# Low parts of the weights by one VectorE instruction per 2048-column tile, and differences of the seven products written over the raw weights

## The chip, the core and the metric

The kernel runs on one core of one Trainium2 chip. The metric is the time of one execution on the device, in microseconds (us); the time of a kernel is the median of its runs. PE is TensorE, DVE is VectorE, ACT is ScalarE, POOL is GpSimd, SP is the engine that issues the transfers from HBM.

## What is computed

A decoder trunk of two layers on 256 tokens of width 2048, all in float32. The reference, cut to what matters here:

```python
for i in range(2):
    h = rms_norm(x, attn_norm[i])
    x = x + (mla_mixer(h, ...) if i == 0 else dilated_mixer(h, ...))
    h = rms_norm(x, ffn_norm[i])
    u = h @ w_up                       # 2048 -> 2 x 5632
    c = conv_b + sum(shift(u, j) * conv_w[j] for j in range(3))
    gate, val = c[..., :5632], c[..., 5632:]
    x = x + (silu(gate) * val) @ w_down
return rms_norm(x, final_norm)
```

Layer 0 mixes tokens by latent attention (16 heads, query and key-value ranks of 512), layer 1 by dilated windows (three groups of 16 heads; its input weights alone are 2048 x 18432). Some 500 MB of weights are read once.

## The kernel before

**Splits.** Every float32 matrix product is made of three passes. A weight tile w, [128, 2048] float32 in pool `wst` (three buffers), is split into a high part wh (ScalarE copies it to float32r) and a low part wl = w - wh (VectorE). Pool `wsp` holds five half tiles of 1024 columns for each of them. The activations have a high and a low part too, side by side in one tile of 512 columns. PE adds xh·wh, xl·wh and xh·wl; with the weights as the stationary operand (`proj`, L116 to L131) a high weight block meets 512 moving columns (both parts of the activations) and a low one 256 (the high part alone). `proj` runs all high blocks of a tile and then all low ones, or the other way round, by turns (`runs`, L110), so that low blocks of two tiles follow each other.

`load` (L71 to L100) issues the transfer on SP and then splits half a tile at a time, ACT on L91, DVE on L92:

```python
for a in range(0, n, WS):
    wh = wsp.tile([P, WS], F32R, name="wh", tag="wh")
    wl = wsp.tile([P, WS], F32R, name="wl", tag="wl")
```

The value half of the latent weights is interleaved instead (L97, L98). `load_tok2` (L133) does the same for the values of the dilated layer, where the weights are the moving operand, 512 columns at a time (`proj_tok2`, L157 to L159).

**Order of the work.** The kernel is written as one sequence, and a compiler pass orders each engine's instructions ahead of time: of what is ready in its own reckoning it takes what stands first in the text, gives each tile one of the buffers of its pool, and puts in the waits. A buffer comes free when all instructions that touch its tile are done. On the chip each engine runs its list in order. `unit` (L195) evacuates the result of one projection after the matmuls of the next. `out_proj` and the last `down` start some projections early, with all but their last columns, and finish them when the last head or gate is ready (L366 to L375, L962 to L969).

**The feed-forward.** 44 blocks of 128 hidden columns, two (gate and value) per block, each an upward projection over 16 chunks (`up`, L946). The downward projection runs in three segments of 14, 14 and 16 blocks, 16 output columns each (`down`, L952). In each layer two groups of four blocks (16 to 19 and 30 to 33) are computed with seven block products in place of eight (`seven`, L817): sums and differences of the 2 x 2 blocks of weights and of activations (`forms`). Six of the products run between the projections of `down` (L974, L975): after each output block one entry of the list first(0), second(0), first(1), ... second(7).

- `first(kk)` loads one weight tile (two transfers, L846); w5[:, i, j] are its four blocks of 512 columns, f by c. ACT makes the high part bh of the two raw blocks with i = 0 (L853), DVE the difference t13 in a tile of its own (L854), ACT its high part ch (L855), DVE the low parts bl (L856) and cl (L857); then 12 matmuls, four products (L826 to L828): two with b, then two with c.
- `second(kk)` makes two more differences in the tile t24 (L865, L866; 512 columns each), the second being the last reader of the raw tile apart from L856, splits them (L867, L868) and runs 6 matmuls, two products.
- `third(q)` (L892), two per group, is the seventh product, whose tile holds four chunks as moving blocks of 512 columns; it runs later, between upward projections (L989).

t13 and t24 have one buffer each (`fpool`).

Of the kernel before, what the change touches and what calls it, by code (L numbers as in the profile page):

```python
# [26 lines left out]
P = 128  # L27
T = 256
# [7 lines left out]
WS = 1024  # L36
# [16 lines left out]
def trunk_kernel(tc, x_d, pos_d, gain_d, conv_d, const_d, mask_d, wqa_d, wkva_d, wqb_d, wkvb_d, wo_d,  # L53
                 win_d, dwo_d, wup_d, wdn_d, out_d):
    nc = tc.nc
    with ExitStack() as ctx:
# [3 lines left out]
        wsp = ctx.enter_context(tc.tile_pool(name="wsp", bufs=5))  # L60
# [10 lines left out]
        def load(src, n, tok=0, cuts=None, after=()):  # L71

            w = wst.tile([P, D], F32, name="w", tag="w")
            cuts = cuts or (0, n)
            for a, b in zip(cuts, cuts[1:]):
                nc.sync.dma_start(w[:, a:b], src[:, a:b])
                if after:
                    after[0]()  # L80
                    after = after[1:]
            parts = []
            for a in range(0, n, WS):
                b = min(n, a + WS)
                wh = wsp.tile([P, WS], F32R, name="wh", tag="wh")
                wl = wsp.tile([P, WS], F32R, name="wl", tag="wl")
                if a < tok:
                    steps = [a] + [c for c in cuts if a < c < b] + [b]
                    for c, e in zip(steps, steps[1:]):
                        h, l = wh[:, c - a:e - a], wl[:, c - a:e - a]  # L90
                        nc.scalar.activation(h, w[:, c:e], AF.Copy)  # L91
                        nc.vector.tensor_sub(l, w[:, c:e], h.bitcast(F32))  # L92
                else:
                    for h, t in enumerate((wh, wl)):
                        src2 = w[:, a + h * WS // 2:a + (h + 1) * WS // 2].rearrange("p (k c) -> p k c", c=T)
                        t4 = t.rearrange("p (k s c) -> p k s c", s=2, c=T)
                        nc.scalar.activation(t4[:, :, 0, :], src2, AF.Copy)  # L97
                        nc.vector.tensor_sub(t4[:, :, 1, :], src2, t4[:, :, 0, :].bitcast(F32))  # L98
                parts.append((wh, wl))
            return parts  # L100
# [15 lines left out]
        def proj(w, xs, n, since=0, upto=None, ps=None):  # L116
# [9 lines left out]
            for i in order:  # L126
                for k in ks:
                    w_k = w[k * P // WS][i][:, k * P % WS:k * P % WS + P]
                    nc.tensor.matmul(ps[:, i * T:], w_k, xs[k][:, :(2 - i) * T], start=(k == 0 and i == own),  # L129
                                     stop=(k == n - 1), skip_group_check=(i != own))  # L130
            return ps  # L131

        def load_tok2(srcs, q):  # L133


            w = wst.tile([P, D], F32, name="w", tag="w")
            for i, src in enumerate(srcs):
                nc.sync.dma_start(w[:, i * WS:(i + 1) * WS], src[q // 2][:, q % 2 * WS:(q % 2 + 1) * WS])
            w4 = w.rearrange("p (i k c) -> p i k c", i=2, c=T)
            parts = []  # L140
            for h in range(2):
                wh = wsp.tile([P, WS], F32R, name="wh", tag="wh")
                wl = wsp.tile([P, WS], F32R, name="wl", tag="wl")
                wh4, wl4 = (t.rearrange("p (k i c) -> p i k c", i=2, c=T) for t in (wh, wl))
                src = w4[:, :, 2 * h:2 * h + 2, :]
                nc.scalar.activation(wh4, src, AF.Copy)  # L146
                nc.vector.tensor_sub(wl4, src, wh4.bitcast(F32))  # L147
                parts += [(wh[:, ts(k, 512)], wl[:, ts(k, 512)]) for k in range(2)]
            return parts
# [11 lines left out]
        def proj_short(w, xs, n, off):  # L161

            ps = pp.tile([P, 512], F32, name="pp", tag="pp")
            for k in range(n):
                a = off + k * P
                wh, wl = (t[:, a % WS:a % WS + P] for t in w[a // WS])
                mm3(ps[:, :T], wh, wl, xs[k][:, :T], xs[k][:, T:], k == 0, k == n - 1)
            return ps[:, :T]

        def proj_tok_short(pieces, xs, tt):  # L170
            ps = pp.tile([P, 512], F32, name="pp", tag="pp")
            n = 4 * len(pieces)
            for k in range(n):
                w = pieces[k // 4][k % 4 // 2][:, k % 2 * 2 * T:(k % 2 + 1) * 2 * T]
                mm3(ps[:, :T], xs[k][:, ts(tt, P)], xs[k][:, T + tt * P:T + (tt + 1) * P],
                    w[:, :T], w[:, T:], k == 0, k == n - 1)
            return ps[:, :T]
# [178 lines left out]
        def out_proj(w_d, os, goff, paired=False, then=None):  # L356
# [9 lines left out]
            while steps:  # L366
# [4 lines left out]
                w = load(w_d[b], D, tok=D)  # L371
# [6 lines left out]
            for b in range(len(early), KC):  # L378
                w = load(w_d[b], D, tok=D)
# [40 lines left out]
        def mla():  # L420
# [49 lines left out]
            for k in range(KC):  # L470

                n = 1 if k < 4 else 2
                if k % 4 == 0:
                    w = wst.tile([P, D], F32, name="w", tag="w")
                if k % 2 == 0:
                    wh = wsp.tile([P, WS], F32R, name="wh", tag="wh")
                    wl = wsp.tile([P, WS], F32R, name="wl", tag="wl")
                c = k % 2 * RANK
# [8 lines left out]
                if k % min(n, 2) == 0:  # L487
                    a = k % 4 * RANK
                    nc.scalar.activation(wh[:, c:c + m], w[:, a:a + m], AF.Copy)
                    nc.vector.tensor_sub(wl[:, c:c + m], w[:, a:a + m], wh[:, c:c + m].bitcast(F32))  # L490
# [18 lines left out]
            for b in range(RC):  # L509
                w = load(wkva_d[b], D, tok=D)  # L510
# [11 lines left out]
            w = load(wkva_d[RC], D, tok=D)  # L522
# [578 lines left out]
```

## Time and profile before

| | us |
|---|---|
| median of 3 runs (2686.86 to 2688.9) | 2687.14 |
| the profiled execution | 2689.23 |
| its span, first to last instruction | 2687.4 |
| PE busy (share of the span) | 2669.4 (99%) |
| weight loads of PE busy | 2353.0 (88%) |
| VectorE busy | 2068.8 (77%) |
| ScalarE busy | 1500.9 (56%) |

The profile is of one execution. A busy time is the union of an engine's instructions; matmuls are pipelined, so that the time from one start to the next says more than the duration of one. A group of instructions has its line, its engine, what it writes and reads by the program's names, their shapes, the count, the total and mean time, and the idle time of the engine just before them with what ended it. wl and wh in a row of `second` or `first` are the halves called bl, cl, dl and bh, ch, dh here; t is t13 or t24.

### The profile page before, as it was taken

The page shows a single profiled execution, that of the slowest core. Times are in us where ns is not written, and L with a number is a line of the kernel's source. Part 1 is how long each engine was busy: PE and PEld are TensorE (multiplying, and loading weights), DVE is VectorE, ACT ScalarE, POOL GpSimd, SP SyncE. Part 2 cuts the span into 40 slices and gives each one's busy share as a digit, 9 for nine tenths or more (in the row PEclk, how much of TensorE's full clock was granted, in tenths as well). Part 3 has the DMA queues.
Part 4 walks back from the last instruction along what each step waited for, and adds up shares of the span by engine and source line. Part 5 has one row for each costly group of instructions (what it writes and reads, how often), then busy time and mean ns, then how long its engine had stood idle before and what let it go on. Part 6 is the DMA issues. An engine that isn't in the chain of part 4 may idle for free.

```text
span 2687.4 us, 39711 instructions
## 1 busy us (share of the span) xinstructions
PE 2669.4 (99%) x15301; PEld 2353.0 (88%) x15301; DVE 2068.8 (77%) x3591; ACT 1500.9 (56%) x2254; POOL 24.4 (1%) x39
## 2 busy tenths in 40 slices
PE   9999999999999999999999999999999999999998
PEld 7998888888888888888888888888888888888887
DVE  7987888789788767676576667667688878978875
ACT  6775666566556554444454454444566646655653
POOL 2000000000000000000000000000000000000000
PEclk9999999999999999999999999999999999999999
DMA  6435555665665555544544544544555566566553
GB/s 236 142 134 204 188 188 184 210 218 186 200 221 192 196 188 191 185 173 170 191 167 165 198 161 173 188 173 160 189 188 189 188 204 219 187 197 225 189 188 126
DMA packets 125902, 501.98 MB, mean 187 GB/s; under 512 B 10000, under 2 KB 60560, under 8 KB 85136
## 3 DMA queue, kind: packets, MB, share of 16 engines
q1 hardware_dynamic: 125424, 499.26, 54.1%
q8 instruction: 120, 1.97, 0.3%
q14 instruction: 70, 0.57, 0.1%
q10 hardware_dynamic: 288, 0.18, 0.0%
HBM read 497.30 MB, written 2.10 MB: 186 GB/s over the span
## 4 chain that ended last, share of the span: by engine, by line
PE 69%; issue 27%; DVE 1%; DMA 1%; POOL 0%; POOLq 0%; ACT 0%; DVEq 0%; SPq 0%; ACTq 0%
PE pp L129 50%; PE pp L157 3%; PE pp L158 3%; PE pp L159 3%; PE pp L104 1%; PE pp L106 1%; PE pp L105 1%; DMA w<-in_wup 1%; PE po L754 1%; PE ps L717 1%; PE ps L826 0%; PE ps L827 0%; PE ps L828 0%; DVE wl L92 0%; PE ps L104 0%
## 5 line engine op out<-in xcount | busy, mean ns | idle before, releaser
L92 DVE TENSOR_TENSOR wl<-w,wh 128x1024 fp32r<-128x1024 f32 (+2 forms) x770 | 912.8, 1193 | 363.8 <-ACT wh L91 234.5
L91 ACT ACTIVATE wh<-w 128x1024 fp32r<-128x1024 f32 (+2 forms) x770 | 793.7, 1034 | 513.2 <-PE pp L129 282.0
L129 PE MATMUL pp<-xs,wh 128*128 128x512 f32 x3904 | 917.5, 390 | 0.0
L129 PEld LDWEIGHTS pp<-xs,wh 128*128 128x128 f32 x3904 | 723.7, 188 | 144.6
L129 PEld LDWEIGHTS pp<-xs,wl 128*128 128x128 f32 x3904 | 487.8, 192 | 9.8
L129 PE MATMUL pp<-xs,wl 128*128 128x256 f32 x3904 | 496.0, 284 | 0.0
L129 PE MATMUL pp<-a,wh 128*128 128x512 f32 x1920 | 454.5, 390 | 0.0
L129 PEld LDWEIGHTS pp<-a,wh 128*128 128x128 f32 x1920 | 357.6, 188 | 72.6
L129 PEld LDWEIGHTS pp<-a,wl 128*128 128x128 f32 x1920 | 244.2, 191 | 9.3 <-DVE wl L92 1.6
L129 PE MATMUL pp<-a,wl 128*128 128x256 f32 x1920 | 248.9, 283 | 0.8 <-DVE wl L92 0.8
L205 ACT ACTIVATE lo<-pp 128x256 f32<-128x256 f32 x241 | 92.5, 384 | 137.2 <-PE pp L129 136.8
L147 DVE TENSOR_TENSOR wl<-w,wh 128x1024 fp32r<-128x1024 f32 x96 | 116.2, 1218 | 62.5 <-ACT wh L146 50.3
L934 DVE SCALAR_TENSOR_TENSOR cv<-upad,convs,cv 128x256 f32<-128x256 f32 x288 | 138.1, 481 | 25.7 <-ACT cv L930 21.5
L146 ACT ACTIVATE wh<-w 128x1024 fp32r<-128x1024 f32 x96 | 101.6, 1058 | 97.0 <-PE pp L158 50.0
L157 PE MATMUL pp<-wh,xs 128*128 128x512 f32 x384 | 150.0, 391 | 0.0
L159 PE MATMUL pp<-wl,xs 128*128 128x512 f32 x384 | 149.4, 389 | 0.0
L158 PE MATMUL pp<-wh,xs 128*128 128x512 f32 x384 | 149.4, 389 | 0.0
L930 ACT ACTIVATE cv<-upad,convs 128x256 f32<-128x256 f32 x144 | 86.1, 599 | 96.8 <-DVE upad L944 95.0
L354 DVE TENSOR_TENSOR x<-x,pp 128x256 f32<-128x256 f32 x256 | 105.2, 414 | 8.2 <-PE pp L129 7.1
L854 DVE TENSOR_TENSOR t<-w 128x1024 f32<-128x1024 f32 x32 | 39.2, 1224 | 82.5 <-DMA w<-in_wup 82.5
L207 DVE TENSOR_TENSOR sum<-pp,lo 128x256 f32<-128x256 f32 x241 | 100.8, 418 | 0.5 <-ACT lo L205 0.4
L159 PEld LDWEIGHTS pp<-wl,xs 128*128 128x128 f32 x384 | 72.1, 188 | 15.1
(291 smaller groups left out, 2630.3 us busy)
## 6 DMA issues: line engine op xcount, KB each, us to landing
w<-in_wup SPq DMA_DIRECT2D x144, 1024.0 KB, 4.8
w<-in_win SPq DMA_DIRECT2D x96, 1024.0 KB, 4.8
w<-in_wdn SPq DMA_DIRECT2D x64, 896.0 KB, 4.6
w<-in_win SPq DMA_DIRECT2D x96, 512.0 KB, 4.1
w<-in_wup SPq DMA_DIRECT2D x64, 512.0 KB, 5.1
w<-in_wdn SPq DMA_DIRECT2D x32, 1024.0 KB, 4.9
w<-in_wo SPq DMA_DIRECT2D x16, 1024.0 KB, 4.8
w<-in_dwo SPq DMA_DIRECT2D x16, 1024.0 KB, 4.8
```

The costliest lines, as they stand in the source:

```text
L91: nc.scalar.activation(h, w[:, c:e], AF.Copy)
L92: nc.vector.tensor_sub(l, w[:, c:e], h.bitcast(F32))
L129: nc.tensor.matmul(ps[:, i * T:], w_k, xs[k][:, :(2 - i) * T], start=(k == 0 and i == own), stop=(k == n - 1), skip_group_check=(i != own))
L146: nc.scalar.activation(wh4, src, AF.Copy)
L147: nc.vector.tensor_sub(wl4, src, wh4.bitcast(F32))
L157: nc.tensor.matmul(ps, xh, wh, start=k == 0, stop=False)
L158: nc.tensor.matmul(ps, xl, wh, start=False, stop=False)
L159: nc.tensor.matmul(ps, xh, wl, start=False, stop=k == KC - 1)
L205: nc.scalar.activation(t, ps[:, T:], AF.Copy)
L207: nc.vector.tensor_add(u, ps[:, :T], t)
L354: nc.vector.tensor_add(x, x, a)
L934: nc.vector.scalar_tensor_tensor(o, v, convs[:, cw + j:cw + j + 1], o, op0=ALU.mult, op1=ALU.add)
```

## The change

- The pool of half tiles is replaced by three high tiles and two low tiles of 2048 columns. `load` splits with two ScalarE instructions and one VectorE instruction over the whole tile. The latent value weights are split like all others and no longer interleaved.
- `load_tok2` and `third` split in the order in which the weights lie, so that a moving block of 512 columns is 2 x 256 or 4 x 128 columns of the tile.
- In `first` the difference t13 is written over the two raw blocks with j = 0, after bh and bl; one of the two differences of `second` is made in `first`, and both lie in the two blocks with j = 1. The high parts b and c are one high tile; their low parts are one tile `scr` with one buffer. `second` takes a high and a low tile. Products 6 and 4 change halves accordingly.
- `sums` and `make_forms` use the same `scr` tile in place of t13 and t24.

```diff
-        wsp = ctx.enter_context(tc.tile_pool(name="wsp", bufs=5))
+        whi = ctx.enter_context(tc.tile_pool(name="whi", bufs=3))
+        wlo = ctx.enter_context(tc.tile_pool(name="wlo", bufs=2))
...
+        def raw_tile():
+            return wst.tile([P, D], F32, name="w", tag="w")
+
+        def high_tile():
+            return whi.tile([P, D], F32R, name="wh", tag="wh")
+
+        def low_tile():
+            return wlo.tile([P, D], F32R, name="wl", tag="wl")
+
+        def halves(w, wh, wl, n):
+
+            for a, b in ((0, D // 2), (D // 2, n)):
+                nc.scalar.activation(wh[:, a:b], w[:, a:b], AF.Copy)
+            nc.vector.tensor_sub(wl[:, :n], w[:, :n], wh[:, :n].bitcast(F32))
+
+        def load(src, n):
+
+            w, wh, wl = raw_tile(), high_tile(), low_tile()
+            nc.sync.dma_start(w[:, :n], src[:, :n])
+            halves(w, wh, wl, n)
+            return wh, wl
...
+            halves(w, wh, wl, D)
+            blocks = [t.rearrange("p (i k c) -> p k i c", i=2, c=T) for t in (wh, wl)]
+            return [tuple(t[:, k] for t in blocks) for k in range(4)]
...
+            def scratch(dtype):
+                return fpool.tile([P, 4 * HALF], dtype, name="scr", tag="scr")
...
-                products = {1: ("a11", 0, 0), 2: ("a12", 0, 1), 5: ("s1", 1, 0), 7: ("s3", 1, 1), 6: ("s2", 2, 0),
-                            4: ("a22", 2, 1)}
+                products = {1: ("a11", 0, 0), 2: ("a12", 0, 1), 5: ("s1", 1, 0), 7: ("s3", 1, 1), 6: ("s2", 2, 1),
+                            4: ("a22", 2, 0)}
...
+                    w, wh, bl = raw_tile(), high_tile(), scratch(F32R)
...
-                    t13 = fpool.tile([P, 2 * HALF], F32, name="t13", tag="t13")
-                    t24 = fpool.tile([P, 2 * HALF], F32, name="t24", tag="t24")
-                    (bh, bl), (ch, cl) = pieces = [pair() for _ in range(2)]
+                    (bh, ch), (bl, cl) = ([t[:, ts(i, 2 * HALF)] for i in range(2)] for t in (wh, bl))
 
                     nc.scalar.activation(as4(bh), w5[:, 0], AF.Copy)
-                    nc.vector.tensor_sub(as4(t13), w5[:, 1], w5[:, :, 0])
-                    nc.scalar.activation(ch, t13, AF.Copy)
                     nc.vector.tensor_sub(as4(bl), w5[:, 0], as4(bh).bitcast(F32))
-                    nc.vector.tensor_sub(cl, t13, ch.bitcast(F32))
+                    t13 = w5[:, :, 0]
+                    nc.vector.tensor_sub(t13, w5[:, 1], t13)
+                    nc.scalar.activation(as4(ch), t13, AF.Copy)
+                    nc.vector.tensor_sub(w5[:, 1, 1], w5[:, 1, 1], w5[:, 0, 0])
+                    nc.vector.tensor_sub(as4(cl), t13, as4(ch).bitcast(F32))
...
-                    nc.vector.tensor_sub(t4[:, 0], w5[:, 1, 1], t1[:, 0])
-                    nc.vector.tensor_sub(t4[:, 1], t4[:, 0], w5[:, 0, 1])
-                    nc.scalar.activation(dh, t24, AF.Copy)
-                    nc.vector.tensor_sub(dl, t24, dh.bitcast(F32))
+                    dh, dl = high_tile()[:, :2 * HALF], low_tile()[:, :2 * HALF]
+
+                    nc.vector.tensor_sub(w5[:, 0, 1], w5[:, 1, 1], w5[:, 0, 1])
+                    t42 = w5[:, :, 1]
+                    nc.scalar.activation(as4(dh), t42, AF.Copy)
+                    nc.vector.tensor_sub(as4(dl), t42, as4(dh).bitcast(F32))
...
-                    for h in range(2):
-                        bh, bl = pair()
-                        as4 = lambda t: t.rearrange("p (k f c) -> p k f c", k=2, f=4)
-                        nc.scalar.activation(as4(bh), w5[:, 2 * h:2 * h + 2], AF.Copy)
-                        nc.vector.tensor_sub(as4(bl), w5[:, 2 * h:2 * h + 2], as4(bh).bitcast(F32))
-                        for k in range(2):
-                            product(3, "s4", 4 * q + 2 * h + k, bh[:, ts(k, HALF)], bl[:, ts(k, HALF)])
+                    halves(w, wh, wl, D)
+                    blocks = [t.rearrange("p (f k c) -> p k f c", f=4, k=4) for t in (wh, wl)]
+                    for k in range(4):
+                        product(3, "s4", 4 * q + k, *(t[:, k] for t in blocks))
```

## Rows read from the trace of the kernel before

**Rows 1.** The page, parts 1 and 2: busy time by engine, granted clock in 40 slices.

```profile
PE 2669.4 (99%) x15301; PEld 2353.0 (88%) x15301; DVE 2068.8 (77%) x3591; ACT 1500.9 (56%) x2254; POOL 24.4 (1%) x39
...
PEclk9999999999999999999999999999999999999999
```

**Rows 2.** Waits of PE and of its weight loads: total us, times, longest.

```profile
PE po L275 <- DVE acc L249: 1.6, 1, 1.6
...
PEld pp L828 <- DVE wl L868: 1.8, 4, 0.5
...
PEld pp L129 <- DVE wl L92: 1.6, 4, 0.5
```

**Rows 3.** Chain that ended last, its longest piece: start us, us, what.

```profile
188.41 84.75 PE pp L129 x488
```

**Rows 4.** Groups by line and shape: count, busy us and mean ns, idle before.

```profile
L129 PE MATMUL pp<-xs,wh 128*128 128x512 f32 x3904 | 917.5, 390 | 0.0
L92 DVE TENSOR_TENSOR wl<-w,wh 128x1024 fp32r<-128x1024 f32 x698 | 849.1, 1221 | 362.9 <-ACT wh L91 233.6 <-PE pp L129 124.0 <-issue 0.5
...
L129 PEld LDWEIGHTS pp<-xs,wh 128*128 128x128 f32 x3904 | 723.7, 188 | 144.6
...
L157 PE MATMUL pp<-wh,xs 128*128 128x512 f32 x384 | 150.0, 391 | 0.0
...
L354 DVE TENSOR_TENSOR x<-x,pp 128x256 f32<-128x256 f32 x256 | 105.2, 414 | 8.2 <-PE pp L129 7.1
...
L854 DVE TENSOR_TENSOR t<-w 128x1024 f32<-128x1024 f32 x32 | 39.2, 1224 | 82.5 <-DMA w<-in_wup 82.5
...
L853 ACT ACTIVATE wh<-w 128x1024 fp32r<-128x1024 f32 x32 | 34.0, 1063 | 33.4 <-PE pp L129 28.3 <-ACT wh L91 3.4 <-ACT cv L930 1.6
...
L92 DVE TENSOR_TENSOR wl<-w,wh 128x512 fp32r<-128x512 f32 x8 | 5.5, 688 | 0.8 <-ACT wh L91 0.8
```

**Rows 5.** Timeline of PE, 451 to 465 us (start, us, what).

```profile
451.02 0.40 PE L826 MATMUL ps<-wh,xs 128*128 128x512 f32 x1
...
453.77 3.33 PE L129 MATMUL pp<-a,wh 128*128 128x512 f32 x14
456.94 1.84 PE L129 MATMUL pp<-a,wl 128*128 128x256 f32 x14
458.61 0.40 PE L826 MATMUL pp<-wh,forms 128*128 128x512 f32 x1
...
464.85 0.40 PE L826 MATMUL ps<-wh,xs 128*128 128x512 f32 x1
```

**Rows 6.** Timeline of DVE, 450 to 466 us.

```profile
450.21 1.23 DVE L854 TENSOR_TENSOR t<-w 128x1024 f32<-128x1024 f32 x1 [0.80 <-DMA w<-in_wup]
...
457.10 0.68 DVE L865 TENSOR_TENSOR t<-w,t 128x512 f32<-128x512 f32 x1
457.81 0.69 DVE L866 TENSOR_TENSOR t<-t,w 128x512 f32<-128x512 f32 x1
458.42 1.22 DVE L856 TENSOR_TENSOR wl<-w,wh 128x1024 fp32r<-128x1024 f32 x1
...
465.58 1.23 DVE L854 TENSOR_TENSOR t<-w 128x1024 f32<-128x1024 f32 x1 [3.01 <-DMA w<-in_wup]
```

**Rows 7.** Timeline of SP, the transfer of the next products' weights.

```profile
459.67 0.93 SPq L846 DMA_DIRECT2D w<-in_wup  x2
```

**Rows 8.** Busy us by engine in one round of the products (PE, PEld, DVE, ACT).

```profile
451.02:464.85 13.83, 13.83 (x77) 11.99 (x76) 11.52 (x17) 7.20 (x8) 0.00 (x0) 1.00 0.67 210
```

**Rows 9.** Windows of 2 us after a wait of PE; the clock follows POOL.

```profile
50.00:52.00 2.00, 2.00 (x16) 2.00 (x16) 1.86 (x5) 1.57 (x3) 0.70 (x1) 0.82 0.00 0
52.00:54.00 2.00, 2.00 (x12) 2.00 (x11) 1.95 (x5) 0.00 (x0) 0.00 (x0) 0.50 0.65 138
54.00:56.00 2.00, 2.00 (x14) 1.91 (x14) 1.89 (x6) 1.31 (x3) 0.00 (x0) 0.83 0.62 255
```

**Rows 10.** Windows of the latent-attention heads.

```profile
80.00:100.00 20.00, 20.00 (x174) 20.00 (x174) 18.96 (x68) 15.52 (x50) 0.00 (x0) 1.00 0.54 186
```

More of the change, by code (lines that the diff above doesn't have):

```diff
@@ L35 @@
 HEADS = 16
-WS = 1024
 NG = 3
@@ L68, in trunk_kernel @@
         pso = ctx.enter_context(tc.tile_pool(name="pso", bufs=1, space=PSUM))
[L71 to L100, printed above, removed]
+        def raw_tile():
[13 more added lines that the diff above has]
+            return wh, wl
         def mm3(ps, ah, al, bh, bl, first, last):
@@ L127, in proj @@
                 for k in ks:
-                    w_k = w[k * P // WS][i][:, k * P % WS:k * P % WS + P]
-                    nc.tensor.matmul(ps[:, i * T:], w_k, xs[k][:, :(2 - i) * T], start=(k == 0 and i == own),
+                    nc.tensor.matmul(ps[:, i * T:], w[i][:, ts(k, P)], xs[k][:, :(2 - i) * T], start=(k == 0 and i == own),
                                      stop=(k == n - 1), skip_group_check=(i != own))
@@ L133, in load_tok2 @@
         def load_tok2(srcs, q):
-            w = wst.tile([P, D], F32, name="w", tag="w")
+            w, wh, wl = raw_tile(), high_tile(), low_tile()
             for i, src in enumerate(srcs):
-                nc.sync.dma_start(w[:, i * WS:(i + 1) * WS], src[q // 2][:, q % 2 * WS:(q % 2 + 1) * WS])
-            w4 = w.rearrange("p (i k c) -> p i k c", i=2, c=T)
-            parts = []
-            for h in range(2):
[L142 to L149, printed above, removed]
+                nc.sync.dma_start(w[:, ts(i, D // 2)], src[q // 2][:, ts(q % 2, D // 2)])
+            halves(w, wh, wl, D)
+            blocks = [t.rearrange("p (i k c) -> p k i c", i=2, c=T) for t in (wh, wl)]
+            return [tuple(t[:, k] for t in blocks) for k in range(4)]
         def proj_tok2(w, pss_, xs, q):
@@ L164, in proj_short, with proj_tok_short @@
             for k in range(n):
-                a = off + k * P
-                wh, wl = (t[:, a % WS:a % WS + P] for t in w[a // WS])
+                wh, wl = (t[:, off + k * P:off + (k + 1) * P] for t in w)
                 mm3(ps[:, :T], wh, wl, xs[k][:, :T], xs[k][:, T:], k == 0, k == n - 1)
             return ps[:, :T]
-        def proj_tok_short(pieces, xs, tt):
+        def proj_tok_short(w, xs, tt, off):
             ps = pp.tile([P, 512], F32, name="pp", tag="pp")
[L172 to L176, printed above, removed]
+            for k in range(RC):
+                wh, wl = (t[:, off + k * T:off + (k + 1) * T] for t in w)
+                mm3(ps[:, :T], xs[k][:, ts(tt, P)], xs[k][:, T + tt * P:T + (tt + 1) * P], wh, wl,
+                    k == 0, k == RC - 1)
             return ps[:, :T]
@@ L370, in out_proj @@
                 b = len(early)
-                w = load(w_d[b], D, tok=D)
+                w = load(w_d[b], D)
                 early.append((w, proj(w, os, KC, upto=HEADS - 2)))
@@ L473, in mla @@
                 if k % 4 == 0:
[L474 to L478, printed above, removed]
+                    w, wh, wl = raw_tile(), high_tile(), low_tile()
+                c = k % 4 * RANK
                 if k % n == 0:
@@ L520, in keep_kpe @@
                 split_to(kpes, kpe)
-            w = load(wkva_d[RC], D, tok=D)
+            w = load(wkva_d[RC], D)
             flush()
@@ L539, in project @@
             def project(j):
-                wq = load(wqb_d[j], 3 * RC * P, tok=D)
-                wkv = load(wkvb_d[j], 4 * RC * P, tok=WS)
+                wq = load(wqb_d[j], 3 * RC * P)
+                wkv = load(wkvb_d[j], 4 * RC * P)
                 h = {}
@@ L583, in project @@
                     unit(lambda: proj_short(wkv, st["skvn"], RC, e * RC * P), lambda ps, e=e: keep_k(e, ps))
[L584 to L585 removed]
+                unit(lambda: proj_tok_short(wkv, st["skvn"], 0, 2 * RC * P), keep_v0)
+                unit(lambda: proj_tok_short(wkv, st["skvn"], 1, 2 * RC * P), keep_v1)
                 return h
@@ L828, in product @@
                     nc.tensor.matmul(ps[i], xh, wl, start=False, stop=(kk == KC // 2 - 1))
-                def pair():
-                    wh = wsp.tile([P, WS], F32R, name="wh", tag="wh")
-                    wl = wsp.tile([P, WS], F32R, name="wl", tag="wl")
-                    return wh, wl
                 raw = {}
@@ L878, in sums @@
                 def sums():
-                    a = fpool.tile([P, 2 * HALF], F32, name="t13", tag="t13")
-                    b = fpool.tile([P, 2 * HALF], F32, name="t24", tag="t24")
-                    u[1, 2], u[2, 2], u[1, 1], u[2, 1] = a[:, :HALF], a[:, HALF:], b[:, :HALF], b[:, HALF:]
+                    a = scratch(F32)
+                    u[1, 2], u[2, 2], u[1, 1], u[2, 1] = (a[:, ts(i, HALF)] for i in range(4))
                     nc.scalar.activation(u[1, 2], ps[1], AF.Copy)
```

39 lines of the change are left out of this document (17 added, 22 removed).

## The prediction

> **What bounds the kernel now.** I read the busy shares first: PE is busy 99% of the span, VectorE (DVE) 77%, and the granted clock is at full speed in every slice [rows 1]. Busy alone doesn't say that PE sets the time, so I read its waits next: everything that PE or its weight loads waited for from the two lines that make low parts, L92 and L868, is 1.6 and 1.8 us, a few tenths at a time [rows 2]. Then the chain that ended last: its longest piece is 488 matmuls in 84.75 us with nothing else in it, 174 ns each; they are half 512 and half 256 columns wide, so a pair takes 347 ns [rows 3]. PE issues matmuls back to back, and the other engines only have to stay ahead. So what the change can give is what PE waits for, about 3.4 us; what it can cost is whatever makes PE wait.
>
> The change touches two things that keep the others ahead: how many weight tiles are in flight, and what must follow what around the seven products. There a round (first and second of one kk, each followed by one block of the downward projection over 14 chunks) takes 13.83 us, PE busy throughout, VectorE 11.52 [rows 8]. With t = 0 at the first product: first(kk) to 2.75, a projection to 7.59, second(kk) to 8.98, a projection to 13.83 [rows 5].
>
> **The change part by part.**
>
> *One VectorE instruction per tile.* 1024 columns take 1221 ns, 512 take 688 [rows 4]: 1.041 ns a column and 155 ns fixed. There were 898 low-part instructions (770 on L92, 16 on L98, 96 on L147, 16 on L906); there will be 445, one per tile: 309 full L92 tiles, 64 of 1792 columns, 16 in the latent heads, 48 value tiles, 8 third products. 453 x 0.155 = 70 us of VectorE work go, but off the path: PE's 3.4 us of waits are the whole cover to be lifted. I take 0, ends 0 and -3.4.
>
> *Later first use.* A low part now exists only when its whole tile is done: 155 + 2048 x 1.041 = 2.29 us after its high part instead of 1.22. In the plain upward stage a projection is 16 x 347 ns = 5.55 us and a low tile is freed a whole projection before its successor is read, so the 2.29 us lie beside PE. Nothing, as long as VectorE isn't late; if it is, 1.07 us per late tile.
>
> *Two low tiles, three high tiles* in place of five halves of each. Cover is lost where a low tile is held longer or freed just before the next is due: (a) the tiles started early before the last head or last gate is ready (L366 to L375, L962 to L969), which keep both low tiles until their last columns run, four places; (b) the fourth projection after each group of seven, whose low tile comes free only one third(q) (12 matmuls, about 2.75 us) before it is due, four places; (c) the latent heads, where VectorE is busy 18.96 of 20 us [rows 10] and the wkv tile's low part now has to fall between the end of one head pair and the fourth unit of the next (36 matmuls of about 0.12 us plus attention). Each costs between 0 and one whole low part, 2.29 us: 4 + 4 + 7 places, 0 to 34 us. I take 0.2 us each, nearer to nothing, since today's waits of this kind are at most 0.5 us [rows 2]: 3 us.
>
> *Differences in place.* Same count of VectorE and ScalarE instructions, but a new order: the 1-3 difference (L854) overwrites raw weights, so it now waits for the high part of the raw weights and its low part (L853, L856). Today it runs straight off the transfer, at 450.21 for products that start at 464.85, over 14 us ahead [rows 5, 6], and this lead hides the wait for the weights that VectorE shows (3.01 us a round, 82.5 in all [rows 4, 6]). And the raw tile, today given back after L856 at 459.64, whereupon the next transfer starts at 459.67 and lands at 465.58, 5.9 us later [rows 6, 7], is now held until second(kk)'s low part. What is queued behind: on SP the next projection's transfer, on VectorE everything after bl.
>
> The round by hand, from rows 4 and 6: the second low tile frees at t = 7.59 when the middle projection ends; the next projection's low part (1792 columns, 2.02 us) ends at 9.6, one residual pair (2 x 0.41) at 10.4. Then bl 1.22, difference 1.22, ch on ScalarE 1.06, cl 1.22: 15.1. The next first(kk) starts at 13.83 and its ninth matmul, eight times 0.229 later (2.75 / 12), is the first to read cl: 15.66. Slack 0.5 us. If the short subtraction (0.69) and dh (1.06) fit beside ch, dl follows cl at once, and the next transfer (5.9) and high part (1.06) are done before 10.4: no wait. If one more residual pair falls into the chain (0.83), PE waits 0.3 us. If the following projection's low part is put ahead of second(kk), dl ends at 15.1 + 2.02 + 0.69 + 1.06 + 1.22 = 20.1; a transfer that has to wait for that raw tile lands at 26.0, 12.2 of the next round, cl is done at 18.0, and PE waits 2.3 us. Ends 0 (PE has next to no wait here to give back) and 2.3 us a round, 32 rounds, 28 of them with a predecessor: 0 to 64 us. I take 0.3, nearer to the first, because in today's order L865 and L866 of second() already run before L856 of first() [rows 6], so the subtractions are issued as soon as they can be: 32 x 0.3 = 10 us.
>
> *Strided moving operands.* Value tiles and third products now give PE 2 x 256 and 4 x 128 columns in place of 512 in a row. No row shows such a read; every 512-column matmul takes 390 or 391 ns [rows 4]. I take 0. As an upper end, each further piece costs the part of a matmul that doesn't shrink with its columns: 14 matmuls of 512 columns go in 3.17 us and 14 of 256 in 1.67 [rows 5], 226 and 119 ns each, so 107 for 256 columns and 12 fixed; (1152 + 3 x 96) x 12 = 17 us.
>
> Sum: 0 + 3 + 10 = +13. The profiled execution took 2689.23 us (span 2687.4), 2.1 over the median of 2687.14; added to the median: **2700 us**. 0.2%, about what measuring this kernel can tell from no change, is 5.4 us.
>
> **The rivals.**
>
> *No change* (2684 to 2692). The chain keeps its 0.5 us, the subtractions fit beside ch, and the edges are covered; a low tile taken from whichever frees first helps. For it: VectorE has 2.3 us idle in a round [rows 8], and the change lightens it by 0.3. Against: the lead of 14 us is gone. 2687. Chance 0.36.
>
> *The raw tile's loop* (the 2.3 us case). Place: the transfer on SP behind dl. It decides once dl ends later than about t = 17.3, so that transfer and high part run past 10.4. 28 x 2.3 + 3 = 2754; partly, 2720 to 2754. A wait of 1.6 us can also cost clock: after the one of that length before L275 [rows 2] the granted clock is 0.82, 0.50 (1.2 of 2.4 GHz) and 0.83 in three windows of 2 us [rows 9], 1.7 us of issue lost; on top of every round this would be 48 more. Chance 0.14.
>
> *PE reads pieces slower*: 2687 + 17 + 13 = 2717. Nothing for it but that nothing rules it out. Chance 0.04.
>
> *Faster: VectorE was the real limit.* If PE's 99% were padding, the 70 us taken off VectorE would return in part; half would give 2652. The rows speak against it: weight loads last 188 ns [rows 4] under matmuls issued 226 ns apart, so their idle share is only the wider matmul streaming. If only the 3.4 us of waits come back it is 2684, which counts as no change. Chance 0.04.
> The Trainium skill (Perfetto Trace Analysis, Identifying the Most-Contended Engine) says that matmul busy time is no measure of headroom and that the weight-load share is; by that the 88% here would leave PE 334 us, and this rival would be likely. The piece of 488 matmuls without a wait disagrees, so I follow the row.
>
> **How the numbers follow.** Forecast (small waits at the products, 2693 to 2720) 0.42; with the loop 0.14 and the slower reads 0.04, slower is 0.60; no change 0.36; faster 0.04. The range, 2684 to 2735, takes in no change, the forecast with the slower reads, and the smaller half of the loop; it leaves out faster and the full loop. The forecast case alone: 2693 to 2720.
>
> **What would show it.** Right: L92's successor at about 2.29 us, VectorE busy down by up to 70 us, rounds of 14.1 to 14.3 us with PE waiting for the low or high part of the difference, and the transfer of in_wup issued right after second()'s low part. Wrong: rounds still at 13.83 (no change), rounds of 15 us or more with the transfer in the chain or the clock below 1 (the loop), or value-tile matmuls issued over 235 ns apart (reads). A span under 2680 would overturn the reading that PE bounds.

## The result, and the profile after the change

The changed kernel takes **2691.91 us** (median of 19 runs, 2690.18 to 2693.96); the kernel before, beside it, 2687.14 (19 runs, 2684.73 to 2689.73): ratio 1.0018, 95% interval 1.0012 to 1.0024. It is 4.8 us slower, just under the 5.4 us that the prediction called no change, and 8 us under its 2700. The profiled execution took 2693.96 us, its span is 2692.2, also 4.8 more than before.

The page's busy times and clock [rows 1]:

```profile
PE 2670.5 (99%) x15301; PEld 2352.7 (87%) x15301; DVE 2015.0 (75%) x3138; ACT 1431.1 (53%) x2246; POOL 19.7 (1%) x39
...
PEclk9999999999999999999999999999999999999999
```

VectorE has 453 instructions fewer, as counted, and 53.8 us less to do; PE is as busy as it was. Groups by line and shape [rows 4]:

```profile
L84 DVE TENSOR_TENSOR wl<-w,wh 128x2048 fp32r<-128x2048 f32 x373 | 853.4, 2288 | 287.4 <-PE pp L119 130.1 <-PE pp L141 110.2 <-ACT v L663 24.8
...
L139 PE MATMUL pp<-wh,xs 128*128 128x512 f32 x384 | 150.1, 391 | 0.0
...
L84 DVE TENSOR_TENSOR wl<-w,wh 128x1792 fp32r<-128x1792 f32 x64 | 129.2, 2019 | 0.0
```

The whole low part takes the 2.29 and 2.02 us worked out, and a value tile's matmul, now reading 2 x 256 columns, 391 ns as before. PE's and the weight loads' waits [rows 2]:

```profile
PE pp L119 <- DVE wl L84: 5.3, 6, 1.5
...
PEld pp L119 <- DVE wl L84: 6.3, 8, 1.8
```

Low parts that PE waits for are few again, but longer: the weight loads' waits reach 1.8 us where the longest was 0.5, PE's own 1.5. The next three views are one round of the seven products. PE's timeline (start, us, what) [rows 5]:

```profile
495.54 0.40 PE L809 MATMUL ps<-wh,xs 128*128 128x512 f32 x1
...
497.83 0.39 PE L811 MATMUL pt<-scr,forms 128*128 128x512 f32 x1
...
498.28 3.34 PE L119 MATMUL pp<-a,wh 128*128 128x512 f32 x14
...
509.36 0.40 PE L809 MATMUL ps<-wh,xs 128*128 128x512 f32 x1
```

From the first product of this round (495.54) to that of the next (509.36) it is 13.82 us: no round is late. 497.83 is the first matmul that reads cl. VectorE's timeline [rows 6]:

```profile
494.39 2.02 DVE L84 TENSOR_TENSOR wl<-w,wh 128x1792 fp32r<-128x1792 f32 x1
496.33 1.22 DVE L835 TENSOR_TENSOR scr<-w,wh 128x1024 fp32r<-128x1024 f32 x1
...
499.69 1.23 DVE L846 TENSOR_TENSOR wl<-w,wh 128x1024 fp32r<-128x1024 f32 x1 [0.88 <-ACT wh L845]
502.75 1.22 DVE L829 TENSOR_TENSOR scr<-w,wh 128x1024 fp32r<-128x1024 f32 x1 [1.83 <-ACT wh L828]
503.89 2.02 DVE L84 TENSOR_TENSOR wl<-w,wh 128x1792 fp32r<-128x1792 f32 x1
```

L829 is bl, L835 cl, L846 dl; cl is done at 497.55, 0.28 us before it is read. A window of one round's length [rows 8]:

```profile
496.23:510.06 13.83, 13.83 (x75) 11.99 (x74) 11.12 (x13) 6.65 (x7) 0.00 (x0) 1.00 0.65 208
```

VectorE is busy 11.12 us of it. SP's timeline [rows 7]:

```profile
496.44 0.93 SPq L824 DMA_DIRECT2D w<-in_wup  x2
...
510.27 0.93 SPq L824 DMA_DIRECT2D w<-in_wup  x2
```

The transfer starts as the neighbouring projection's low part ends (494.39 + 2.02 = 496.41), and 3.3 us before dl begins. So it seems to take that projection's raw tile and not to wait for its predecessor's; experiments 1 and 6 bear this out.

Where the 4.8 us come from, by the same PE instruction in both traces (the first matmul of a round's third product, `pt`): the seven rounds from the first round's mark to the last's take 96.82, 98.17, 96.79 and 98.49 us in the four groups before, 96.83, 96.83, 96.85 and 96.83 after, **2.9 us less**. The stretches outside take 3.0 (up to the first group), 0.9, 2.0, 1.2 and 0.6 us more, **7.7 us**. The waits shown next make 5.7 of it. The other 2.0 are not explained; a second profile of the kernel before (experiment 10) differs from the first by as much there. PE's timeline there, all stretches between single rows left out:

```profile
77.27 0.38 PE L95 MATMUL pp<-sqh,wl 128*128 128x256 f32 x1 [0.42 <-DVE k L321]
...
192.56 1.94 PE L119 MATMUL pp<-a,wl 128*128 128x256 f32 x14 [1.45 <-DVE wl L84]
...
583.00 1.22 PE L119 MATMUL pp<-xs,wl 128*128 128x256 f32 x8 [0.54 <-DVE wl L84]
...
813.03 2.17 PE L119 MATMUL pp<-xs,wl 128*128 128x256 f32 x16 [0.56 <-DVE wl L84]
...
927.61 1.66 PE L119 MATMUL pp<-a,wl 128*128 128x256 f32 x12 [1.24 <-DVE wl L84]
...
2263.55 1.69 PE L119 MATMUL pp<-xs,wl 128*128 128x256 f32 x12 [1.07 <-DVE wl L84]
...
2606.63 1.54 PE L119 MATMUL pp<-a,wl 128*128 128x256 f32 x11 [0.44 <-DVE wl L84]
```

192.56, 927.61 and 2606.63 are the prediction's place (a), tiles started early; 583.00, 813.03 and 2263.55 its place (b), the fourth projection after a group. VectorE's timeline at the first of each:

```profile
189.65 0.42 DVE L321 TENSOR_TENSOR a<-pt,a 128x256 fp32r<-128x256 f32 x1
190.21 2.29 DVE L84 TENSOR_TENSOR wl<-w,wh 128x2048 fp32r<-128x2048 f32 x1
...
579.27 1.00 DVE L907 SCALAR_TENSOR_TENSOR cv<-upad,convs,cv 128x256 f32<-128x256 f32 x2 [1.66 <-ACT cv L903]
580.31 0.42 DVE L912 TENSOR_TENSOR cv<-cv 128x256 f32<-128x256 f32 x1
580.66 2.29 DVE L84 TENSOR_TENSOR wl<-w,wh 128x2048 fp32r<-128x2048 f32 x1
```

PE goes on as soon as the whole 2.29 us are over. The low part could not start earlier at 190.21: both low tiles were held by the early projections, and PE came to the last low block of the first of them only at 189.89. At 580.66 it could have: by the order of use its tile was free from about 579.7 on (PE read the projection before from 577.63 for 2.08 us), but L907 and L912, which had waited for ScalarE, stand ahead of it in VectorE's list.

### The profile page after: what moved, and what is told of

The parts are those of the page before. It is cut to its first block, busy times and chain, and to the rows that moved or that the text cites. A ratio compares the mean times of both kernels' runs of the same rounds, so it can differ in the third digit from the quotient of the medians.

```text
span 2692.2 us, 38702 instructions
## 1 busy us (share of the span) xinstructions
PE 2670.5 (99%) x15301; PEld 2352.7 (87%) x15301; DVE 2015.0 (75%) x3138; ACT 1431.1 (53%) x2246; POOL 19.7 (1%) x39
## 4 chain that ended last, share of the span: by engine, by line
PE 68%; issue 27%; DVE 2%; DMA 1%; ACT 0%; POOLq 0%; POOL 0%; DVEq 0%; ACTq 0%
PE pp L119 49%; PE pp L139 3%; PE pp L141 3%; PE pp L140 3%; DVE wl L84 1%; PE pp L95 1%; PE pp L97 1%; PE pp L96 1%; PE ps L694 1%; DMA w<-in_wup 1%; PE po L731 1%; PE ps L97 0%; PE ps L95 0%; PE ps L96 0%; PE ps L809 0%
## 5 line engine op out<-in xcount | busy, mean ns | idle before, releaser
L84 DVE TENSOR_TENSOR wl<-w,wh 128x2048 fp32r<-128x2048 f32 (+2 forms) x445 | 996.7, 2240 | 289.4 <-PE pp L119 130.1
L83 ACT ACTIVATE wh<-w 128x1024 fp32r<-128x1024 f32 x890 | 884.7, 1031 | 410.3 <-PE pp L119 136.1
L119 PEld LDWEIGHTS pp<-xs,wl 128*128 128x128 f32 x3904 | 486.7, 192 | 14.1 <-DVE wl L84 4.2
L907 DVE SCALAR_TENSOR_TENSOR cv<-upad,convs,cv 128x256 f32<-128x256 f32 x288 | 138.2, 482 | 61.4 <-ACT cv L903 55.7
L829 DVE TENSOR_TENSOR scr<-w,wh 128x1024 fp32r<-128x1024 f32 x32 | 39.2, 1226 | 61.5 <-ACT wh L828 61.5
L139 PEld LDWEIGHTS pp<-wh,xs 128*128 128x128 f32 x384 | 72.1, 188 | 14.8
L140 PEld LDWEIGHTS pp<-wh,xs 128*128 128x128 f32 x384 | 72.1, 188 | 14.8
```

The costliest lines, as they stand in the source:

```text
L83: nc.scalar.activation(wh[:, a:b], w[:, a:b], AF.Copy)
L84: nc.vector.tensor_sub(wl[:, :n], w[:, :n], wh[:, :n].bitcast(F32))
L119: nc.tensor.matmul(ps[:, i * T:], w[i][:, ts(k, P)], xs[k][:, :(2 - i) * T], start=(k == 0 and i == own), stop=(k == n - 1), skip_group_ch ...
L139: nc.tensor.matmul(ps, xh, wh, start=k == 0, stop=False)
L140: nc.tensor.matmul(ps, xl, wh, start=False, stop=False)
L829: nc.vector.tensor_sub(as4(bl), w5[:, 0], as4(bh).bitcast(F32))
```

## The experiments

Two theories stood against each other for the 7.7 us: whole tiles (a low part is one long instruction, of which nothing can be read before its end), or the number of low buffers and the order. For the rounds the question was why the 10 us were not there. Each ratio is to the kernel before, run beside the experiment; its median was 2685.33 us beside experiments 1 to 4, 2686.94 beside 5 to 8 and 2687.45 beside 9 and 10.

**1. The low part in two instructions, same tiles.**

```diff
             for a, b in ((0, D // 2), (D // 2, n)):
                 nc.scalar.activation(wh[:, a:b], w[:, a:b], AF.Copy)
-            nc.vector.tensor_sub(wl[:, :n], w[:, :n], wh[:, :n].bitcast(F32))
+                nc.vector.tensor_sub(wl[:, a:b], w[:, a:b], wh[:, a:b].bitcast(F32))
```

> The changed kernel, but the low part of each loaded tile is made by two VectorE instructions of one half each; the two whole low tiles stay. Theory A (the loss is PE waiting for the last 1.07 us of a low part that now comes in one piece): the six waits of PE for low parts (1.45, 0.54, 0.56, 1.24, 1.07 and 0.44 us in the profile of the changed kernel, 5.3 in all) shrink by up to 1.07 each to about 0.4 in all, and the time falls by 4 to 5 us to about 2687. Theory B (the loss is that a whole low tile has to come free first): the waits move by a few tenths only, and the time stays at 2690 to 2692. VectorE is busier by about 60 us in either case.

Measured: 2698.47 us (5 runs), 1.0052 (1.0040 to 1.0064). The edge waits shrank (at the first place from 1.45 to 0.38), and yet it is slower: the rounds now last up to 14.9 us, 9.6 us more in the four groups. The timeline of one of them, all engines:

```profile
481.56 0.93 SPq L824 DMA_DIRECT2D w<-in_wup  x2
...
493.19 1.22 DVE L84 TENSOR_TENSOR wl<-w,wh 128x1024 fp32r<-128x1024 f32 x1
...
494.33 1.22 DVE L835 TENSOR_TENSOR scr<-w,wh 128x1024 fp32r<-128x1024 f32 x1
...
495.46 0.96 DVE L84 TENSOR_TENSOR wl<-w,wh 128x768 fp32r<-128x768 f32 x1
495.61 0.50 PE L811 MATMUL pt<-scr,forms 128*128 128x512 f32 x1 [0.81 <-DVE scr L835]
...
496.48 0.93 SPq L824 DMA_DIRECT2D w<-in_wup  x2
...
500.88 1.06 ACT L828 ACTIVATE wh<-w 128x1024 fp32r<-128x1024 f32 x1 [0.67 <-DMA w<-in_wup]
```

The order puts cl between the two halves of the neighbour's low part, so that its raw tile comes free 1.1 us later; the transfer starts when it does (495.46 + 0.96 = 496.42), ACT waits for the transfer, and bl, cl and the next round follow. Two transfers stand 14.92 us apart here, 13.83 in the changed kernel. So the round can be late in the way the prediction priced, through a raw tile, but the neighbour's. cl's place alone is not enough for it, as experiment 2 shows.

**2. Low tiles of half the size, four in place of two.**

```diff
-        wlo = ctx.enter_context(tc.tile_pool(name="wlo", bufs=2))
+        wlo = ctx.enter_context(tc.tile_pool(name="wlo", bufs=4))
...
-            return wlo.tile([P, D], F32R, name="wl", tag="wl")
+            return wlo.tile([P, D // 2], F32R, name="wl", tag="wl")
...
-            nc.vector.tensor_sub(wl[:, :n], w[:, :n], wh[:, :n].bitcast(F32))
+                nc.vector.tensor_sub(wl[i][:, :b - a], w[:, a:b], wh[:, a:b].bitcast(F32))
```

> The changed kernel with four low half tiles of 1024 columns in place of two whole ones (the same memory), each filled by an instruction of its own and freed by itself. Theory A and theory B both expect the six waits for low parts to go (5.3 us) and the time to fall to 2684 to 2687; if two low tiles are not the reason (the three high tiles, or the order of ScalarE's copies, or the reads of the moving operand in pieces), the time stays at 2690 to 2692.

Measured: 2685.58 us (median of 12 runs, 2684.93 to 2686.26 but for one of 8047.19), 1.0001 (0.9992 to 1.0010). Of the edge waits one is left (1.03 us at 196.49), and all rounds but one (14.12) last 13.83. The same bytes, released and filled in halves, cost nothing: it is the size of the unit that costs, not the space. VectorE in a round that is on time:

```profile
721.30 1.23 DVE L84 TENSOR_TENSOR wl<-w,wh 128x1024 fp32r<-128x1024 f32 x1 [0.72 <-ACT wh L83]
...
723.05 1.22 DVE L854 TENSOR_TENSOR scr<-w,wh 128x1024 fp32r<-128x1024 f32 x1
724.18 0.95 DVE L84 TENSOR_TENSOR wl<-w,wh 128x768 fp32r<-128x768 f32 x1
```

cl (L854) stands between the neighbour's halves here too. But one half of a projection's low part is made between bl and cl, where experiment 1 has three: the two halves of the other projection are made ahead of bl (those at 728.42 and 730.52 ahead of bl at 731.72).

**3. The order of high and low blocks after the third products.** `proj` alternates high-low and low-high; this starts it with high blocks after a third product.

```diff
                         product(3, "s4", 4 * q + k, *(t[:, k] for t in blocks))
+                    state["run"] = 0
```

> The changed kernel, but the projection after each third product begins with its high part. If the three waits of 0.54, 0.56 and 1.07 us after the groups of seven come from a low tile that is freed one third product before it is due, they go, and the time falls by about 2 us to 2690; the waits at 192.6, 927.6 and 2606.6 us stay. If something else is late there, nothing changes.

Measured: 2695.80 us (5 runs), 1.0040 (1.0028 to 1.0052). The three waits of place (b) are gone, but everything behind alternates the other way round, and places (a) pay for it. PE's timeline at one:

```profile
915.22 2.08 PE L119 MATMUL pp<-a,wl 128*128 128x256 f32 x16
...
919.68 3.43 PE L119 MATMUL pp<-a,wl 128*128 128x256 f32 x16 [1.80 <-DVE wl L84]
```

The windows behind it (busy us of PE, PEld, DVE, ACT and POOL, then the granted clock, the share of the DMA engines, GB/s):

```profile
920.00:922.00 2.00, 2.00 (x12) 2.00 (x11) 2.00 (x4) 2.00 (x4) 0.00 (x0) 0.54 0.69 193
922.00:924.00 2.00, 2.00 (x10) 1.82 (x9) 2.00 (x4) 0.92 (x3) 0.00 (x0) 0.61 0.81 336
```

The wait is 1.80 us instead of 1.24, and behind it the granted clock is near its lower level, 1.2 of 2.4 GHz: the 16 matmuls take 3.43 us, where the 16 before the wait take 2.08.

**4. The differences over the raw weights alone.** The kernel before, five half tiles each, with the change's `first` and `second` (its own low tiles for b and c kept).

```diff
-                    nc.vector.tensor_sub(as4(t13), w5[:, 1], w5[:, :, 0])
-                    nc.scalar.activation(ch, t13, AF.Copy)
                     nc.vector.tensor_sub(as4(bl), w5[:, 0], as4(bh).bitcast(F32))
-                    nc.vector.tensor_sub(cl, t13, ch.bitcast(F32))
+                    t13 = w5[:, :, 0]
+                    nc.vector.tensor_sub(t13, w5[:, 1], t13)
+                    nc.scalar.activation(as4(ch), t13, AF.Copy)
+                    nc.vector.tensor_sub(w5[:, 1, 1], w5[:, 1, 1], w5[:, 0, 0])
+                    nc.vector.tensor_sub(as4(cl), t13, as4(ch).bitcast(F32))
```

> The kernel before with its five half tiles of each kind; only the differences of the seven products are written over the raw weights. The recorded prediction priced this part at 0.3 us a round, 10 us in all: 2697. By the two traces it is a gain: the last two rounds of the second and the fourth group took 14.4 to 14.8 us before and 13.84 after, 2.9 us less, so about 2684, with no round over 13.9. If those late rounds were cured by the shorter low parts or the new pools instead, it stays at 2687.

Measured: 2684.58 us (11 runs), 0.9998 (0.9989 to 1.0006), and every round 13.82 or 13.83. The part that was to cost 10 us costs nothing.

**5. Two instructions everywhere but beside the products.**

```diff
-                    w = load(wdn_d[layer, c, :, a * P:b * P], n * P)
+                    w = load(wdn_d[layer, c, :, a * P:b * P], n * P, one=bool(mains))
```

(`halves` makes one low part if `one`, two otherwise.)

> The changed kernel, with the low part of a weight tile again made by two VectorE instructions (1024 columns each, into the same whole low tile), except for the tiles of the downward projections that stand between the seven products, which keep the one instruction. Theory A (two instructions shorten the waits at the edges, but one instruction beside the products is what lets the raw tile go early enough for the next transfer): the rounds stay at 13.83 us, the seven rounds' span of a group at 96.8 us instead of the 98.6 to 99.7 of the kernel with two instructions everywhere, and the edge waits are the short ones of that kernel; about 3.4 us less than the changed kernel, 2687 to 2689 us. Theory B (the late rounds came from somewhere else, for instance from VectorE's 155 ns for every further instruction): rounds of 14.1 to 14.9 us again, 2695 to 2699 us. Theory C (the edges don't matter, the waits there are taken out of later ones): like the changed kernel, 2691 to 2693 us.

Measured: 2687.35 us (11 runs), 1.0000 (0.9991 to 1.0008). Rounds of 13.83 and the short edge waits. VectorE in a round:

```profile
505.32 2.02 DVE L87 TENSOR_TENSOR wl<-w,wh 128x1792 fp32r<-128x1792 f32 x1
507.26 1.22 DVE L838 TENSOR_TENSOR scr<-w,wh 128x1024 fp32r<-128x1024 f32 x1
```

cl (L838) can no longer come between. With whole low tiles the single instruction is what keeps the round on time, and what costs at the edges: without it there, the change is as fast as the kernel before.

**6. The products' raw tile in a pool of its own**, one buffer; two for all other raw tiles.

```diff
-        wst = ctx.enter_context(tc.tile_pool(name="wst", bufs=3))
+        wst = ctx.enter_context(tc.tile_pool(name="wst", bufs=2))
+        wsf = ctx.enter_context(tc.tile_pool(name="wsf", bufs=1))
```

> The changed kernel, with the raw tile of the six products in a pool of its own with one buffer, and two buffers instead of three for all other raw tiles, so that the next transfer of these weights has to wait for the low part of second() (it ends at 500.9 us in the round of the changed kernel whose next transfer starts at 496.44). Theory A (the loop through the raw tile doesn't bind in the changed kernel only because the next transfer takes whichever of three buffers comes free first, here that of the neighbouring projection): the transfer starts some 4.5 us later, the high part of the raw weights too, and the rounds are 15.5 to 18 us; 28 rounds with a predecessor, 50 to 115 us more, 2740 to 2810 us. Theory B (the transfer has slack enough anyway): rounds of 13.83 us and 2690 to 2694 us.

Measured: 2749.17 us (4 runs), 1.0228 (1.0214 to 1.0242). Now the transfer does wait for dl (L847), and ACT for the transfer (timeline, all engines):

```profile
502.23 1.23 DVE L847 TENSOR_TENSOR wl<-wf,wh 128x1024 fp32r<-128x1024 f32 x1 [0.88 <-ACT wh L846]
...
503.49 0.93 SPq L825 DMA_DIRECT2D wf<-in_wup  x2
...
507.74 1.06 ACT L829 ACTIVATE wh<-wf 128x1024 fp32r<-128x1024 f32 x1 [3.86 <-DMA wf<-in_wup]
```

Two of PE's waits, total us, times, longest:

```profile
PE pp L120 <- DVE wl L85: 17.1, 8, 3.3
PE pt L812 <- DVE scr L836: 15.9, 26, 0.8
```

That is the loop of the prediction's second rival, and its place is right, but most rounds became 14.7 to 15.1 us, not 15.5 to 18: 27.6 us in the four groups. PE waits for cl in 26 rounds, 15.9 us; how much of the rest is the loop and how much the lack of a third raw buffer for the projections is not separated. The other 26 us of the span are outside the rounds, where only the third raw buffer is missing, among them a wait of 3.3 us behind each group. It costs clock as well: in the 2 us from 594.00, right behind the first of these waits, the granted clock is 0.50, and it falls to that level behind the other three too.

**7 and 8. One more VectorE instruction in each round**: half of bl, or all of it, a second time.

```diff
                     nc.vector.tensor_sub(as4(bl), w5[:, 0], as4(bh).bitcast(F32))
+                    nc.vector.tensor_sub(as4(bl)[:, 0], w5[:, 0, 0], as4(bh)[:, 0].bitcast(F32))
```

> The changed kernel, with one more VectorE instruction of 512 columns (0.69 us) in each round: half of the low part of the raw weights is made a second time, with the same values, right behind the first. It measures the slack of the chain bl, difference, ch, cl. Theory A (the low part cl, done 0.5 us before its first matmul, is the tightest point of the round and all VectorE work ahead of it delays it): PE waits about 0.2 us for it, the rounds are 14.0 us, 5 to 7 us more in all, 2696 to 2699 us. Theory B (the 1.83 us for which VectorE waits in the round before bl can be used, since the order is adapted): rounds of 13.83 us, 2690 to 2694 us.

> The changed kernel, with one more VectorE instruction of 1024 columns (1.22 us) in each round: the whole low part of the raw weights is made a second time, with the same values, right behind the first. Theory A (0.5 us of slack before cl's first matmul, all VectorE work ahead of it delays it): PE waits 0.7 us a round, rounds of 14.5 us, 20 us more in all, 2709 to 2714 us. Theory B (VectorE's idle 2.7 us of a round take it up): rounds of 13.83 us, 2690 to 2694 us.

Measured: 2698.83 us (4 runs), 1.0048 (1.0034 to 1.0062) for the half, 2697.34 (5 runs), 1.0038 (1.0025 to 1.0051) for the whole. In the profiles the four groups take 4.9 and 8.3 us more than in the changed kernel, 0.17 and 0.30 for each of 28 rounds. The half's sum is near theory A's 5 to 7 us, but two rounds of 15.1 us make half of it; the whole cost less than half of its 0.7 a round. Neither measures the slack of the old chain alone, for both lists were laid anew: in most rounds a projection's low part stands ahead of bl (502.12 and 504.39 with the half, 502.75 and 505.02 with the whole), which in the changed kernel stands behind it (503.89, bl 502.75). Neither is free although VectorE is idle for 2.7 us of a round (13.83 less the 11.12 that it is busy).

**9. Whole tiles alone**: the differences in t13 and t24 as before, b's and c's low parts in one of the two low tiles.

```diff
-                    w, wh, bl = raw_tile(), high_tile(), scratch(F32R)
+                    w, wh, bl = raw_tile(), high_tile(), low_tile()
```

> The other half of the change alone: whole high and low tiles with one VectorE instruction everywhere, but the differences of the seven products in tiles of their own again (t13, t24), straight off the transfer, and the low parts b and c of a round in one of the two low tiles instead of in a tile of their own. Theory A (two low tiles are the narrow place wherever more than two weight tiles follow closely): in a round four low tiles pass through two buffers; the one behind second() is freed 1.4 us before the next projection begins and takes 2.02 us, so PE waits up to 0.6 us a round, 0 to 17 us over 28 rounds on top of the edge waits of the changed kernel: 2693 to 2712 us. Theory B (what costs in the changed kernel is the difference made over the raw weights; with the lead of the differences back nothing is late): rounds of 13.83 us and 2686 to 2692 us.

Measured: 2707.16 us (5 runs), 1.0073 (1.0059 to 1.0087), PE's waits:

```profile
PE pp L119 <- DVE wl L84: 13.6, 20, 1.6
```

The rounds take 11.0 us more than in the changed kernel. The time lies in theory A's range, but the trace shows another cause than its two low tiles. VectorE and PE at one of the waits:

```profile
777.88 1.23 DVE L832 TENSOR_TENSOR t<-w 128x1024 f32<-128x1024 f32 x1 [3.57 <-DMA w<-in_wup]
...
780.48 2.02 DVE L84 TENSOR_TENSOR wl<-w,wh 128x1792 fp32r<-128x1792 f32 x1
...
782.55 1.93 PE L119 MATMUL pp<-a,wl 128*128 128x256 f32 x14 [0.88 <-DVE wl L84]
```

PE had read the last of dl at 778.11, so that both low tiles were free some 2 us before the low part began at 780.48. What stood ahead of it in VectorE's list is the difference straight off the transfer (L832), which had waited 3.57 us, and the two short ones behind it. All twelve waits in the rounds look like this, the difference waiting 2.98 to 4.28 us each time. So the two parts belong together: alone the first costs 20 us and the second nothing, together they cost 5, for the differences in place take that wait out of the list. They also leave 8 KB a partition for `scr`, a third place for low parts in a round; what this is worth no run shows.

**10. The kernel before, a second profile.**

> The kernel before once more, for a second profile. Theory A (its late rounds at the end of the second and the fourth group, 14.44 to 14.75 us, come from the order of its instructions and are there in each execution): the same four rounds are late by the same amounts, in all 2.9 us, and the span is 2687 us. Theory B (they belong to the one profiled execution, for instance to a transfer that landed late): rounds of 13.83 us throughout and a span of about 2684 us, which would also say that the changed kernel's rounds gained nothing.

Measured: 2686.84 us, span 2685.1. Neither theory: rounds are late again, but others, the last of each group (14.88, 13.99, 15.10 and 14.16), 2.6 us in all over the changed kernel's rounds, against 2.9 in the first profile. The timeline in the late one of the first group, PE and VectorE:

```profile
537.27 1.23 DVE L854 TENSOR_TENSOR t<-w 128x1024 f32<-128x1024 f32 x1 [4.11 <-DMA w<-in_wup]
...
538.41 0.95 DVE L92 TENSOR_TENSOR wl<-w,wh 128x768 fp32r<-128x768 f32 x1
...
539.42 0.98 PE L129 MATMUL pp<-a,wl 128*128 128x256 f32 x6 [0.49 <-DVE wl L92]
```

L854, the difference straight off the transfer, stands ahead of the neighbour's low part in VectorE's list. Where it waits 4.11 us for its transfer, and not 3.01 [rows 6], the low part behind it comes late, and PE waits. No round is late like this in the profile of the change, nor in that of experiment 4; the late rounds of experiment 9, which has this difference again, are.

## Why the prediction was right or wrong

**PE sets the time: right.** 53.8 us less work on VectorE gave nothing back. The 70 us were 453 times 155 ns; measured are 119 ns each, for an instruction begins before its predecessor's time is over (503.89 after 502.75 + 1.22 = 503.97), so part of the fixed cost was already hidden. The weight loads' 87%, which the Trainium skill (Perfetto Trace Analysis, Identifying the Most-Contended Engine) takes, next to the rate of arithmetic, as a measure of headroom, told no more here than the 88% before: the trace goes on disagreeing.

**Reads in pieces: right**, 391 ns [rows 4], and the value tiles' matmuls are issued 227 ns apart in the mean of both traces, short of the 235 that would have spoken against it.

**Later first use: right**, nothing in the plain upward stage; one late step at 77.27, where k was behind a low part in one piece (74.46, 1.75 us): 0.42 us.

**Two low tiles at the edges: the mechanism and two of its three places right, the size wrong.** It said 0.2 us a place, 3 us. Six of the eight places (a) and (b) wait, 5.3 us together, 0.9 us each; the heads, 7 of the 15 places, have only the 0.42; and the stretches outside the rounds lose 7.7 us. The step that failed is the choice between the ends: it took the waits of before [rows 2], which are those of half tiles, as the nearest row. At 192.56 PE waits from 191.11 on for a low part that began at 190.21, so the price is the whole low part less what PE still had to do, and that is nearer to the upper end. Experiment 2 gives it back, the 2.0 us without a named wait too.

**Differences in place: +10 predicted, -2.9 measured in the rounds of the profiles. This is the term that was mis-sized, to the wrong side of nothing**, for three reasons. First, the chain by hand went by the matmul order of before: cl at 15.1, read at 15.66. On the chip cl is done at t = 15.84 (497.55 - 495.54 + 13.83), 0.74 later, just as the step feared, with other work of VectorE between (in the lines above the neighbour's low part at 494.39). But the compiler also moved cl's readers, from the ninth matmul to the eleventh, 16.12. Of 0.5 us slack 0.28 are left, not -0.3. Second, the transfer isn't behind dl: it takes whichever of three raw tiles is free first. Third, it priced the lead of L854 as cover that is lost. In VectorE's list it is also a wait for a transfer, ahead of a low part that PE needs next; the late round shown in experiment 10 comes from it, and so do the waits in the rounds of experiment 9; late rounds cost the kernel before 2.6 and 2.9 us in its two profiles. That the late rounds go away with the in-place differences is seen in one profile of experiment 4; the medians of the runs, 0.75 us apart, don't resolve it (the interval goes from 2.9 us less to 1.6 more).

The 0.3 us a round was a fair size for a round in which this chain is late: experiments 1, 7 and 8 make the rounds late by 0.34, 0.17 and 0.30 us on the mean of 28, through cl or through what it is made from. What failed is that the change as written pays it.

**The rivals.** The time lies at the upper edge of "no change" (2684 to 2692), but by two terms of opposite sign, not by covered edges. The raw tile's loop exists and was off: experiment 6 shows its place and 1 us a round. Nothing came back from VectorE, and the reads cost nothing. The signs asked for: the 2.29 us are there; rounds of 14.1 to 14.3 and the transfer behind dl are not.

**Open:** where 2.0 of the 7.7 us outside the rounds go, and what the differences in place alone are worth in timed runs. That experiment 8 costs less than experiment 7 in timed runs isn't shown: the intervals of their ratios overlap.

## What to carry to other kernels

Fewer and longer instructions on an engine that is off the path save work that nobody waits for, and make each release and each first use later: look for the places where a held buffer meets its next use, and price them one by one with the whole new duration, not with the waits of the old grain. A chain worked out by hand in the old order is a bound, not a forecast, where a compiler lays all lists anew: it can move the readers too. And an early instruction that waits for a transfer isn't only a lead; ask what stands behind it in its engine's list. In experiment 9 that was the low part that PE waited for, in all twelve waits within the rounds.

## What the hardware showed that was not expected

A wait can cost more than itself in clock: in experiment 3 after 1.80 us without a matmul two windows of 2 us have a granted clock of 0.54 and 0.61, and 16 matmuls take 1.35 us more; after the 1.24 us at the same place in the changed kernel the matmuls go on at full pace (12 in 1.66 us). Behind the waits of 3.3 us in experiment 6 the same happens each time. Reading the moving operand in two or four pieces of a tile costs nothing that shows: 512 columns are issued 227 ns apart in the value tiles either way, and 228 in the third products.
